# Up projection's seven-product tiles: products in more PSUM banks, closing sums last, two of the token sums split on GpSimd

## The chip, the cores and the metric

The kernel runs on one core of one Trainium2 chip. The metric is the device time of one execution in microseconds (us). Engines are named as the profile names them: PE is the TensorE matmul engine and PEld its weight load, DVE is VectorE, ACT is ScalarE, POOL is GpSimd, SP is SyncE, which issues the loads. Results of matmuls land in PSUM, which this kernel allots as eight banks of 128 partitions by 512 fp32.

## The reference

One layer of a hybrid network over 512 tokens of width 1024: a state-space mixer and a sparse attention mixer side by side, a feed-forward block with a causal convolution, and a gated embedding. What the change touches is the first half of the feed-forward block:

```
hid = rmsnorm(h, g_ffn) @ w_up          # 512x1024 @ 1024x5632
hid = causal_conv(hid, width 3) + conv_b
a, b = split(hid, 2)                     # 2816 columns each
h = h + (gelu(a) * b) @ w_down
```

All of it is fp32. The kernel splits every fp32 operand of a matmul into a high and a low part (high = the value rounded to the matmul's format, low = the rest) and sums three matmuls, high by high, high by low and low by high.

## The kernel before, in words

The stages before the feed-forward block (projections, state-space scan, attention, merge, output projection) end with the normed tokens `n2h`, `n2l` (high and low, 128 partitions by 8 row blocks by 512 tokens). The up projection then runs over 22 tiles `f` of 128 hidden columns; a tile makes the a-half and the b-half of its columns, each 128 by 512 tokens, in two PSUM banks called `ua` and `ub`.

**Plain tiles.** 17 of the 22 tiles load two raw weight blocks of 128 by 1024 (`wr`, three buffers), split each into `wh` and `wl` (two buffers each; the copy that makes the high part is always on ACT, the subtraction that makes the low part on DVE for the a-half and on POOL for the b-half), and run 8 times 3 matmuls of 512 columns into `ua`, then the same into `ub`.

**Seven-product tiles.** For `f` = 4, 6, 8, 10 and 12 (`SEVEN`) the function `up_seven` treats the tile as a 2 by 2 block product (a-half and b-half columns by the two halves of the 1024 rows, times the two token halves) and uses the Strassen-Winograd form: seven block products of 4 times 3 matmuls of 256 columns, in place of eight. Its inputs are sums of weight blocks, made for each tile in `weight_sums` (s1 to s4 in tiles `sf`, split into `sw`), and sums of token blocks, made once in `token_sums` during tile 1 (`nf`, split into `nt`). The products come in the order 1, 2, 6, 7, 5, 3, 4, each into half a bank (`H0` or `H1`, 256 columns). Products 1 and 7 share bank C, 6 is in bank D (both called `us`), products 2 and 3 share the a-bank `ua`, products 5 and 4 the b-bank `ub`. An ACT copy takes product 1 to `m1`; DVE sums make u2 = p6 + m1, u3 = p7 + u2, u4 = p5 + u2 (tiles `mu`), and four closing sums in place, p2 += m1, p5 += u3, p3 += u4, p4 += u3, leave the a-half in `ua` and the b-half in `ub`.

**After a tile** the function `convolved` reads both banks: ACT scales each into `cv`, DVE adds two shifted terms for each half (`scalar_tensor_tensor`, line 63), ACT applies gelu, POOL multiplies (later tiles in two pieces), ACT and DVE split the product into `ffp` (pairs of tiles 0 to 7) or `ffa` and `ffs` with more sums (from tile 8).

**PSUM.** The pool has four tags of two banks each: `acc`, `s`, `t` and `o`. A tag's two banks are taken in turn. `either()` gives `acc` and `o` in turn; every tile takes its `ua` bank from `either()` and its `ub` bank from `s`; a seven-product tile takes C and D from `t`.

**Order.** On PE the instructions run in the order of the program from tile 2 on (`manual_schedule`). On ACT, DVE, POOL and the load queue a planner orders them at build time: it simulates the engines, and takes among the ready instructions the one that stands earliest in the program. `issue_after(x)` puts the instructions traced within it behind `x` where both are on one engine. Once built, each engine runs its list strictly in that order and waits at the head for whatever is not there yet. A wait between engines on a PSUM tile covers the bank: the profile shows PE waiting for a sum in the other half of the bank that it is to write.

In the profile the splits show as line 75 (ACT copy) and line 54 (all `tensor_tensor`), matmuls as lines 82 to 84, the convolution's shifted terms as line 63, its scaled copy as line 1360 and gelu as line 1363.

Of the kernel before, what the change touches and what calls it, by code (L numbers as in the profile page):

```python
# [16 lines left out]
MUL, ADD, SUB = ALU.mult, ALU.add, ALU.subtract  # L17

P = 128
# [3 lines left out]
KD = D // P  # L23
# [21 lines left out]
def hybrid_kernel(ctx: ExitStack, tc: tile.TileContext, A, out):  # L45
    nc = tc.nc
    V, G, S, PE = nc.vector, nc.gpsimd, nc.scalar, nc.tensor
# [5 lines left out]
    def tt(o, a, b, op, e=V):  # L53
        e.tensor_tensor(o, a, b, op=op)  # L54
# [19 lines left out]
    def copy(o, a):  # L74
        S.activation(o, a, AF.Copy)  # L75

    def split(hi, lo, src, e=V):
        copy(hi, src)
        tt(lo, src, hi, SUB, e)

    def mm3(ps, lh, ll, rh, rl, start, stop):
        PE.matmul(ps, lh, rh, start=start, stop=False)  # L82
        PE.matmul(ps, lh, rl, start=False, stop=False)  # L83
        PE.matmul(ps, ll, rh, start=False, stop=stop)  # L84
# [15 lines left out]
    def bank(tag, name):  # L100
        return psp.tile([P, 512], F32, tag=tag, name=name, bufs=BANKS[tag])
# [71 lines left out]
    def last(engine):  # L173
        return next(i for i in reversed(nc.cur_bb.bb.instructions) if i.engine == engine)
# [3 lines left out]
    def either():  # L178
        turn[0] ^= 1
        return ("acc", "o")[turn[0]]  # L180

    def wraw(name, ld, row0, c0, kt, c, raw=None):

        if raw is None:
            raw = pw.tile([P, kt * c], F32, name="wr", tag="wr", bufs=3)
            raw = raw.rearrange("p (k c) -> p k c", k=kt)
        n = (row0 // (kt * P)) * (ld // c) + c0 // c
        nc.sync.dma_start(raw, dr(name, n * P * kt * c, [[kt * c, P], [c, kt], [1, c]]))
        return raw

    def wload(name, ld, row0, c0, kt, c, e=V, keep=None, raw=None):
        if raw is None:
            raw = wraw(name, ld, row0, c0, kt, c)
        if keep is None:
            hi = pw.tile([P, kt * c], F32R, name="wh", tag="wh").rearrange("p (k c) -> p k c", k=kt)
            lo = pw.tile([P, kt * c], F32R, name="wl", tag="wl").rearrange("p (k c) -> p k c", k=kt)
        else:
            hi, lo = keep
        split(hi, lo, raw, e)
        return hi, lo  # L200
# [506 lines left out]
    for lv in range(5):  # L707
        n = 1 << lv
        m = MID + n
        rotate([t[:, :, m:m + n] for t in tab], [t[:, :, MID:m] for t in tab], n, lv, [t[:, :, :n] for t in tabm], G)  # L710
    for t, c, sign in zip(tab, (COS, SIN), (1.0, -1.0)):
        S.activation(t[:, :, 0], c[:, 6], AF.Copy, scale=sign)
        x = t[:, :, HC - 1:HC]
# [308 lines left out]
    for hc in range(2):  # L1022
# [3 lines left out]
        for cc in range(2):  # L1026
            c = 2 * hc + cc
            ps = bank(either(), "glu")
# [169 lines left out]
    for d2 in range(4):  # L1198
        hi, lo = wload("w_br_nsa", D, 0, d2 * 256, 4, 256, V)
        for dd in range(2):  # L1200
            dt_ = 2 * d2 + dd
            ps = bank(either(), "br")
# [24 lines left out]
    for qp in range(2):  # L1227
        for hf, qt in ((0, 0), (0, 1), (1, 0), (1, 1)) if qp == 0 else ((0, 2), (1, 2), (0, 3), (1, 3)):
            cs = slice(hf * 512, hf * 512 + 512)
            qs_ = slice(qt * P, (qt + 1) * P)  # L1230
            ps = bank(either(), "wo")
# [109 lines left out]
    ups = {}  # L1341

    def up(f, t0, t1_):
        wab, pss = ups[f]
        for ab in range(2):
            hi, lo = wab[ab]
            for k in range(KD):
                mm3(pss[ab][:, t0:t1_], hi[:, k], lo[:, k], n2h[:, k, t0:t1_], n2l[:, k, t0:t1_],
                    k == 0, k == KD - 1)
# [16 lines left out]
    SEVEN = range(4, 13, 2)  # L1366
    K1, K2, H0, H1 = slice(0, 4), slice(4, 8), slice(0, HT), slice(HT, T)
    BT = {}

    def token_sums():  # L1370
        n = {}
        for ks, hs in ((K1, H0), (K2, H0), (K1, H1), (K2, H1)):
            t = Slot("nf", 2)
            tt(t.parts(4), n2h[:, ks, hs], n2l[:, ks, hs], ADD, G)
            n[ks.start, hs.start] = t
        n11, n21, n12, n22 = (t.parts(4) for t in n.values())
        tt(n11, n12, n11, SUB)
        tt(n12, n22, n12, SUB)
        tt(n22, n22, n11, SUB)
        tt(n21, n21, n22, SUB)  # L1380
        for m, x in ((6, n22), (7, n12), (5, n11), (4, n21)):
            w = 4 if m == 4 else 2
            BT[m] = [[Slot("nt", w // 2, F32R) for _ in range(4 // w)] for _ in range(2)]
            for i in range(4 // w):
                split(*(BT[m][y][i].parts(w) for y in range(2)), x[:, w * i:w * i + w])
        for t in n.values():
            t.done()

    def tokens(m, x, k):
        if m in BT:  # L1390
            w = 4 // len(BT[m][x])
            return BT[m][x][k // w].parts(w)[:, k % w]
        ks, hs = {1: (0, H0), 2: (4, H0), 3: (4, H1)}[m]
        return (n2h, n2l)[x][:, ks + k, hs]

    def weight_sums(f):
        raw = [wraw("w_up", 2 * DFF, 0, ab * DFF + f * P, KD, P) for ab in range(2)]
        a11, a12, a21, a22 = (r[:, ks] for r in raw for ks in (K1, K2))
        sf = [Slot("sf", 2) for _ in range(2)]
        (s1, s2), (s3, s4) = ([v.rearrange("p (k c) -> p k c", k=4) for v in (t.t[:, :512], t.t[:, 512:])] for t in sf)  # L1400
        tt(s1, a21, a22, ADD)
        tt(s2, s1, a11, SUB)
        tt(s3, a11, a21, SUB)
        tt(s4, a12, s2, SUB)
        wa = wload(None, 0, 0, 0, KD, P, V, raw=raw[0])
        wb = [pw.tile([P, 4, P], F32R, name=n, tag=n) for n in ("wh", "wl")]
        split(*wb, a22, G)
        hl = [[Slot("sw", 2, F32R) for _ in range(2)] for _ in range(2)]
        for i in range(2):
            split(hl[i][0].t, hl[i][1].t, sf[i].t, (V, G)[i])  # L1410
            sf[i].done()
        W = {1: [w[:, K1] for w in wa], 2: [w[:, K2] for w in wa], 4: wb}
        for m, (i, o) in {5: (0, 0), 6: (0, 4), 7: (1, 0), 3: (1, 4)}.items():
            W[m] = [t.parts(8)[:, o:o + 4] for t in hl[i]]
        return W, [t for x in hl for t in x]

    def up_seven(f):
        W, held = weight_sums(f)
        A, B = ups[f][1]
        C, D_ = (bank("t", "us") for _ in range(2))  # L1420
        ps = {1: C[:, H0], 2: A[:, H0], 6: D_[:, H0], 7: C[:, H1], 5: B[:, H1], 3: A[:, H1], 4: B[:, H0]}
        u = Slot("mu", 2)
        m1, u2, u3, u4 = (u.parts(4)[:, i] for i in range(4))

        def prod(m):
            for k in range(4):
                mm3(ps[m], W[m][0][:, k], W[m][1][:, k], tokens(m, 0, k), tokens(m, 1, k), k == 0, k == 3)

        prod(1)
        copy(m1, ps[1])  # L1430
        prod(2)
        tt(ps[2], ps[2], m1, ADD)
        prod(6)
        tt(u2, ps[6], m1, ADD)
        prod(7)
        tt(u3, ps[7], u2, ADD)
        prod(5)
        tt(u4, ps[5], u2, ADD)
        tt(ps[5], ps[5], u3, ADD)
        prod(3)  # L1440
        tt(ps[3], ps[3], u4, ADD)
        prod(4)
        tt(ps[4], ps[4], u3, ADD)
        for t in (*held, u):
            t.done()

    def up_tile(f):
        kept = []
        if f == 1:
            kept = [Slot(f"w1{n}", 2, F32R) for n in range(4)]  # L1450
        wab = []
        for ab in range(0 if f in SEVEN else 2):
            keep = [kept[2 * ab + x].parts(KD) for x in range(2)] if kept else None
            wab.append(wload("w_up", 2 * DFF, 0, ab * DFF + f * P, KD, P, (V, G)[ab], keep=keep))
        ups[f] = wab, [bank(either(), "ua"), bank("s", "ub")]
        if f == 0:
            up(0, 0, 256)
            return
        if f == 1:
            up(1, 0, 256)  # L1460
            up(0, 256, 512)
            convolved(0)
            up(1, 256, 512)
            for k_ in kept:
                k_.done()
            token_sums()
        elif f in SEVEN:
            up_seven(f)
            if f == SEVEN[-1]:
                for t in BT.values():  # L1470
                    for x in t:
                        for y in x:
                            y.done()
        else:
            up(f, 0, 512)
        convolved(f)
        if f >= NF - 2:
            free[2].append(cvs[f % 2])

    for f in range(2):  # L1480
        up_tile(f)
    with tc.manual_schedule(engines={mybir.EngineType.PE}):
        for f in range(2, NF):
            up_tile(f)
# [5 lines left out]
    b1, b2, u4, us_at = {}, {}, {}, {}  # L1490
    with tc.manual_schedule(engines={mybir.EngineType.PE}):
# [73 lines left out]
        for n, c in enumerate(range(NR, NP)):  # L1565
# [5 lines left out]
            x = [u[:, n % NSET] for u in (uh, ul)]  # L1571
# [296 lines left out]
```

## Time and profile before

| what | value |
|---|---|
| median of 3 runs | 807.33 us (806.28 to 808.7) |
| profiled execution, its own time | 806.57 us |
| its span, first to last instruction | 804.8 us |
| mean granted PE clock | 0.998 |
| PE busy | 787.4 us (98%), 4618 matmuls |
| DVE, ACT, POOL busy | 578.3, 416.2, 283.2 us |

Up projection in the span: tile 0 starts at 390.3 us, the first seven-product tile at 437.17 us, the last one ends at 541.85 us, the stage ends at about 640 us.

How to read it: all times inside the execution count from the first instruction of the span. In a timeline row the first number is the start, the second the length of the row, and a bracket at the end tells how long the engine sat idle before it and what it waited for. Rows of instructions that follow without a gap overlap a little, since they are pipelined. In a row of a view by stretches the pairs are busy time and, in brackets, the count of instructions of each engine.

### The profile page before, as it was taken

To read this page: it belongs to the slowest core of one execution; us is meant where nothing else is said; L and a number is where in the kernel's file an instruction comes from. 1 tells how busy PE (TensorE), PEld (TensorE's weight loads), DVE (VectorE), ACT (ScalarE), POOL (GpSimd) and SP (SyncE) were. 2 spreads that over 40 slices of the span, in tenths; PEclk is the share of its full clock that TensorE was granted. 3 is DMA by queue.
4 is the path that set the end of the run, shared out by engine and by line. 5 is a ranking of instruction groups with operands and counts; after the bars stand their busy time and mean duration, and the time that the engine had idled before them with its cause. 6 is when DMAs were issued, how large, how long until landed. Compare 5 with 4: busy or idle time off the path is not lost.

```text
span 804.8 us, 12548 instructions
## 1 busy us (share of the span) xinstructions
PE 787.4 (98%) x4618; PEld 671.5 (83%) x4618; DVE 578.3 (72%) x1156; ACT 416.2 (52%) x769; POOL 283.2 (35%) x302
## 2 busy tenths in 40 slices
PE   9999999999999999999999899899999999999996
PEld 8888888878888888878997788788888888888885
DVE  7988987976777730785599888885544757999753
ACT  6836554467767642443464554454443433484642
POOL 4576122137555433311354444553333200001222
PEclk9999999999999999999999999999999999999999
DMA  9973112243135123342032233234232352525111
GB/s 351 354 210 108 53 68 67 67 121 115 54 105 165 46 67 115 113 156 73 1 105 79 79 105 103 81 107 155 82 103 94 98 174 79 209 66 171 53 53 52
DMA packets 29854, 89.72 MB, mean 111 GB/s; under 512 B 3681, under 2 KB 6113, under 8 KB 29793
## 3 DMA queue, kind: packets, MB, share of 16 engines
q1 hardware_dynamic: 29216, 87.88, 33.0%
q10 hardware_dynamic: 576, 1.05, 0.3%
q8 instruction: 36, 0.59, 0.3%
q14 instruction: 26, 0.20, 0.1%
HBM read 79.48 MB, written 5.24 MB: 105 GB/s over the span
## 4 chain that ended last, share of the span: by engine, by line
PE 74%; DVE 14%; ACT 4%; issue 3%; POOL 2%; DMA 2%; POOLq 0%; ACTq 0%; DVEq 0%
PE pj L82 6%; PE pj L83 6%; PE pj L84 6%; PE p L83 3%; PE p L82 3%; PE p L84 3%; DVE wl L54 3%; PE ub L82 2%; PE sps L1068 2%; PE ub L83 2%; PE ub L84 2%; PE ua L83 2%; PE ua L82 2%; PE ua L84 2%; PE ptp L1088 2%
## 5 line engine op out<-in xcount | busy, mean ns | idle before, releaser
L54 POOL TENSOR_TENSOR wl<-wr,wh 128x1024 fp32r<-128x1024 f32 (+1 forms) x39 | 89.8, 2303 | 211.2 <-ACT wh L75 188.8
L75 ACT ACTIVATE wh<-wr 128x1024 fp32r<-128x1024 f32 x88 | 90.9, 1033 | 95.7 <-issue 28.6
L54 DVE TENSOR_TENSOR wl<-wr,wh 128x1024 fp32r<-128x1024 f32 x49 | 71.3, 1454 | 44.9 <-ACT wh L75 44.7
L82 PE MATMUL pj<-n1h,wh 128*128 128x512 f32 x224 | 91.0, 406 | 0.0
L83 PE MATMUL pj<-n1l,wh 128*128 128x512 f32 x224 | 87.7, 392 | 0.0
L84 PE MATMUL pj<-n1h,wl 128*128 128x512 f32 x224 | 87.5, 391 | 0.0
L63 DVE SCALAR_TENSOR_TENSOR cv<-ub,cols,cv 128x511 f32<-128x511 f32 (+1 forms) x44 | 32.9, 747 | 35.7 <-ACT cv L1360 35.0
L83 PE MATMUL ua<-n2l,wh 128*128 128x512 f32 (+1 forms) x156 | 57.0, 366 | 0.2 <-DVE n2l L63 0.2
L82 PE MATMUL ua<-n2h,wh 128*128 128x512 f32 (+1 forms) x156 | 57.1, 366 | 0.0
L84 PE MATMUL ua<-n2h,wl 128*128 128x512 f32 (+1 forms) x156 | 56.9, 365 | 0.0
L84 PE MATMUL ub<-n2h,wl 128*128 128x512 f32 (+1 forms) x136 | 51.3, 377 | 0.0
L83 PE MATMUL ub<-n2l,wh 128*128 128x512 f32 (+1 forms) x136 | 51.2, 377 | 0.0
L82 PE MATMUL ub<-n2h,wh 128*128 128x512 f32 (+1 forms) x136 | 51.2, 377 | 0.0
L84 PEld LDWEIGHTS pj<-n1h,wl 128*128 128x128 f32 x224 | 42.0, 188 | 8.9
L82 PEld LDWEIGHTS pj<-n1h,wh 128*128 128x128 f32 x224 | 42.1, 188 | 8.2 <-issue 0.4
L83 PEld LDWEIGHTS pj<-n1l,wh 128*128 128x128 f32 x224 | 42.2, 188 | 7.3 <-issue 0.2
L60 POOL TENSOR_SCALAR pr<-pr,su,gates 128x512 f32<-128x512 f32 (+2 forms) x64 | 39.1, 626 | 14.2 <-DVE su L1080 14.1
L75 ACT ACTIVATE ph<-ptp 128x128 fp32r<-128x128 f32 (+1 forms) x64 | 27.8, 435 | 25.9 <-PE ptp L1088 25.7
L54 DVE TENSOR_TENSOR pl<-ptp,ph 128x128 fp32r<-128x128 f32 (+1 forms) x64 | 31.0, 486 | 13.3 <-ACT ph L75 12.2
L54 POOL TENSOR_TENSOR cv<-cv 128x256 f32<-128x256 f32 (+1 forms) x22 | 26.6, 1209 | 31.0 <-DVE cv L63 26.7
L1079 ACT ACTIVATE pr<-pr,nb 128x512 f32<-128x512 f32 (+2 forms) x64 | 35.4, 557 | 0.7 <-DVE nb L1077 0.6
L1077 DVE CUSTOM_DVE_ANT_0 pr<-sps,maskb 128x512 f32<-128x512 f32 (+2 forms) x64 | 28.9, 488 | 8.4 <-PE ptp L1088 6.3
(529 smaller groups left out, 2276.1 us busy)
## 6 DMA issues: line engine op xcount, KB each, us to landing
wr<-in_w_up_dram SPq DMA_DIRECT2D x44, 512.0 KB, 3.5
wr<-in_w_in_dram SPq DMA_DIRECT2D x28, 512.0 KB, 3.7
b<-in_w_down_dram SPq DMA_DIRECT2D x14, 512.0 KB, 3.6
QQ<-QT SPq DMA_DIRECT2D x16, 256.0 KB, 4.6
wr<-in_w_out_dram SPq DMA_DIRECT2D x8, 512.0 KB, 3.4
wr<-in_w_down_dram SPq DMA_DIRECT2D x8, 512.0 KB, 4.2
wr<-in_w_ple_gate_dram SPq DMA_DIRECT2D x8, 512.0 KB, 3.5
xT<-in_x_t_dram SPq DMA_DIRECT2D x4, 512.0 KB, 9.8
```

What stands on the lines that cost most here:

```text
L54: e.tensor_tensor(o, a, b, op=op)
L60: e.tensor_scalar(o, a, s1, s2, op0=op0, op1=op1)
L63: e.scalar_tensor_tensor(o, a, s, b, op0=op0, op1=op1)
L75: S.activation(o, a, AF.Copy)
L82: PE.matmul(ps, lh, rh, start=start, stop=False)
L83: PE.matmul(ps, lh, rl, start=False, stop=False)
L84: PE.matmul(ps, ll, rh, start=False, stop=stop)
L1068: PE.matmul(o, self.QQ[:, x, qt * P:(qt + 1) * P], KK[:, :, self.g, :w] if both else KK[:, self.br, self.g, :w], start=x == 0, stop=x == 1)
L1077: V.tensor_tensor_reduce(out=pp, in0=ps, in1=maskb[:, T - w:], scale=-(HD ** -0.5), scalar=3e38, op0=ADD, op1=ALU.min, accum_out=nb)
L1079: S.activation(pp, pp, AF.Exp, bias=nb, scale=-1.0, accum_out=su)
L1088: PE.transpose(ps[:, (qt - kt) * P:(qt - kt + 1) * P], self.pr[qt][:, kt * P:(kt + 1) * P], ident)
```

## The change

Four edits.

1. `token_sums`: the low parts of the token sums for products 4 and 5 (three subtractions, two of 128 by 512 and one of 128 by 1024) move from DVE to POOL.
2. `weight_sums`: the load of `wa` (the split of the first raw block, which products 1 and 2 use) stands ahead of the four weight sums instead of behind them. For the first seven-product tile only, the ACT copies of the `sw` splits are put behind the ACT copy of `wa`.
3. `up_seven`: six banks in place of four. Product 7 goes to a bank of its own, E (from `either()`), product 3 to a bank of its own, X (from `s`), product 5 to the second half of C. `ua` holds product 2 alone and `ub` product 4 alone.
4. The closing sums: p2 + m1 stays in place in `ua`; p3 + u4 is read from X and written to the second half of `ua`; p5 + u3 is read from C and written to the second half of `ub`, after product 4 in the program; p4 + u3 stays in place and comes last.

```
-                split(*(BT[m][y][i].parts(w) for y in range(2)), x[:, w * i:w * i + w])
+                split(*(BT[m][y][i].parts(w) for y in range(2)), x[:, w * i:w * i + w], G if m in (4, 5) else V)
...
     def weight_sums(f):
         raw = [wraw("w_up", 2 * DFF, 0, ab * DFF + f * P, KD, P) for ab in range(2)]
         a11, a12, a21, a22 = (r[:, ks] for r in raw for ks in (K1, K2))
+        wa = wload(None, 0, 0, 0, KD, P, V, raw=raw[0])
+        wa_at = last(mybir.EngineType.Activation)
         sf = [Slot("sf", 2) for _ in range(2)]
...
         tt(s4, a12, s2, SUB)
-        wa = wload(None, 0, 0, 0, KD, P, V, raw=raw[0])
         wb = [pw.tile([P, 4, P], F32R, name=n, tag=n) for n in ("wh", "wl")]
         split(*wb, a22, G)
         hl = [[Slot("sw", 2, F32R) for _ in range(2)] for _ in range(2)]
         for i in range(2):
-            split(hl[i][0].t, hl[i][1].t, sf[i].t, (V, G)[i])
+            with tc.issue_after(wa_at) if f == SEVEN[0] else nullcontext():
+                split(hl[i][0].t, hl[i][1].t, sf[i].t, (V, G)[i])
...
     def up_seven(f):
         W, held = weight_sums(f)
-        A, B = ups[f][1]
+        X, E = bank("s", "us"), bank(either(), "us")
         C, D_ = (bank("t", "us") for _ in range(2))
-        ps = {1: C[:, H0], 2: A[:, H0], 6: D_[:, H0], 7: C[:, H1], 5: B[:, H1], 3: A[:, H1], 4: B[:, H0]}
+        A, B = ups[f][1] = [bank(either(), "ua"), bank("s", "ub")]
+        ps = {1: C[:, H0], 2: A[:, H0], 6: D_[:, H0], 7: E[:, H0], 5: C[:, H1], 3: X[:, H0], 4: B[:, H0]}
...
         prod(2)
-        tt(ps[2], ps[2], m1, ADD)
+        tt(A[:, H0], ps[2], m1, ADD)
...
         prod(5)
         tt(u4, ps[5], u2, ADD)
-        tt(ps[5], ps[5], u3, ADD)
         prod(3)
-        tt(ps[3], ps[3], u4, ADD)
+        tt(A[:, H1], ps[3], u4, ADD)
         prod(4)
-        tt(ps[4], ps[4], u3, ADD)
+        tt(B[:, H1], ps[5], u3, ADD)
+        tt(B[:, H0], ps[4], u3, ADD)
...
-        ups[f] = wab, [bank(either(), "ua"), bank("s", "ub")]
+        ups[f] = [wab, None if f in SEVEN else [bank(either(), "ua"), bank("s", "ub")]]
```

## The prediction, on record before the result

> **What bounds the kernel now.** I read the page first, then the stretches between the starts of the seven-product tiles, then what PE waits for in them, then the timelines around each wait. The page's first line and the stretches (span in us, then busy time and count of PE, PEld, DVE, ACT, POOL, then clock and DMA):
>
> ```profile
> PE 787.4 (98%) x4618; PEld 671.5 (83%) x4618; DVE 578.3 (72%) x1156; ACT 416.2 (52%) x769; POOL 283.2 (35%) x302
> ```
> ```profile
> 437.17:452.00 14.83, 10.87 (x85) 10.26 (x85) 11.32 (x14) 4.84 (x8) 6.66 (x4) 1.00 0.31 107
> 452.00:474.27 22.27, 21.38 (x135) 19.20 (x133) 19.22 (x25) 10.84 (x15) 10.21 (x5) 1.00 0.29 95
> 474.27:496.51 22.24, 21.34 (x134) 19.18 (x133) 19.09 (x24) 10.84 (x15) 10.20 (x5) 1.00 0.29 95
> 496.51:520.47 23.96, 21.61 (x135) 19.24 (x133) 21.23 (x32) 10.94 (x16) 11.45 (x7) 1.00 0.28 89
> 520.47:541.85 21.38, 21.24 (x135) 19.15 (x133) 17.97 (x29) 12.31 (x18) 11.83 (x7) 1.00 0.30 99
> 541.85:640.00 98.15, 98.15 (x435) 81.27 (x434) 52.98 (x82) 42.22 (x60) 34.61 (x27) 1.00 0.31 104
> ```
> ```profile
> PE ub L82 <- DVE ub L54: 4.9, 4, 1.9
> PE us L82 <- ACT mu L75: 1.7, 2, 1.3
> PE us L84 <- DVE wl L54: 1.5, 1, 1.5
> ```
>
> PE is the bound (98% busy, full clock), so a microsecond counts where PE stands still. The first stretch is tile 4 alone; the next four are each a plain tile and a seven-product tile of the same work, yet last 22.27, 22.24, 23.96 and 21.38 us. The last block is all that PE waits for in those stretches: 4.9 + 1.7 + 1.5 = 8.1 us, in seven waits. From 541.85 to 640 PE is busy without a gap, so time won before goes straight to the end.
>
> **The change part by part.** (1) *Products in their own banks.* The wait of product 4 in tile 6, and the DVE queue ahead of it:
>
> ```profile
> 472.73 0.38 PE L82 MATMUL ub<-nt,wh 128*128 128x256 f32 x1 [0.89 <-DVE ub L54]
> ```
> ```profile
> 468.47 2.27 DVE L54 TENSOR_TENSOR wl<-wr,wh 128x1024 fp32r<-128x1024 f32 x1
> ...
> 472.26 0.42 DVE L54 TENSOR_TENSOR ub<-ub,mu 128x256 f32<-128x256 f32 x1
> 474.16 1.29 DVE L54 TENSOR_TENSOR sf<-wr 128x512 f32<-128x512 f32 x2 [1.48 <-DMA wr<-in_w_up_dram]
> 475.37 0.43 DVE L54 TENSOR_TENSOR ua<-ua,mu 128x256 f32<-128x256 f32 x1
> ```
>
> Product 4 goes to the first half of the bank where DVE still sums product 5 in the second half, and that sum stands in DVE's queue behind a weight split of 2.27 us and the sums u2, u3 and u4. After the change the bank holds product 4 alone; nothing of DVE's is due in it before PE writes. The 4.9 us go. Product 7 likewise no longer waits for the ACT copy of product 1 (1.7 us), since it has bank E; product 5 now shares that bank and comes two products later:
>
> ```profile
> 488.17 0.28 PE L82 MATMUL us<-nt,sw 128*128 128x256 f32 x1
> 491.05 0.28 PE L82 MATMUL ub<-nt,sw 128*128 128x256 f32 x1
> ```
>
> Products 6 and 7 lie between these rows, so a product takes 2.88 / 2 = 1.44 us, and the copy has 1.44 us more before it is due. The first matmul after a wait takes 0.38 us against 0.28 here: 0.10 for each of seven restarts, 0.7 us. All waits together are worth 8.1 + 0.7 = 8.8 us. The count of DVE sums stays seven a tile; none is added.
>
> (2) *Tile 4.* One of the waits on DVE's sums (removed above), and these two, with what stood in the queues:
>
> ```profile
> 439.07 0.39 PE L84 MATMUL us<-n2h,wl 128*128 128x256 f32 x1 [1.48 <-DVE wl L54]
> 444.72 0.38 PE L82 MATMUL us<-nt,sw 128*128 128x256 f32 x1 [1.31 <-ACT mu L75]
> ```
> ```profile
> 433.78 1.06 ACT L75 ACTIVATE sw<-sf 128x1024 fp32r<-128x1024 f32 x1 [3.65 <-DVE sf L54]
> ...
> 436.00 1.05 ACT L75 ACTIVATE wh<-wr 128x1024 fp32r<-128x1024 f32 x1
> ...
> 442.58 0.63 ACT L1363 ACTIVATE cv<-cv 128x512 f32<-128x512 f32 x1 [3.98 <-DVE cv L63]
> ...
> 444.30 0.37 ACT L75 ACTIVATE mu<-us 128x256 f32<-128x256 f32 x1
> ```
> ```profile
> 437.08 1.94 DVE L54 TENSOR_TENSOR wl<-wr,wh 128x1024 fp32r<-128x1024 f32 x1 [0.29 <-ACT wh L75]
> ```
> ```profile
> 437.90 3.38 POOL L54 TENSOR_TENSOR sw<-sf,sw 128x1024 fp32r<-128x1024 f32 x1
> ```
> ```profile
> 431.58 0.39 PE L82 MATMUL ub<-n2h,wh 128*128 128x512 f32 x1
> ```
>
> The `wa` copy stood behind both `sw` copies on ACT, which had idled 3.65 us before them. Its buffer comes free when PE leaves the a-half of tile 3 at 431.58. Put first, the copy ends near 431.6 + 0.2 (for the last matmuls to end) + 1.05 = 432.9 and the low part by 432.9 + 1.94 = 434.8, before PE arrives at 437.17: the 1.48 us go. Behind it on ACT wait the two `sw` copies, and behind them POOL's split; the sums keep PE no earlier than product 6 at 437.17 + 2.88 = 440.05.
>
> What is late next is product 5, due at 437.17 + 4 x 1.44 = 442.93, while the ACT copy of product 1 ended at 444.30 + 0.37 = 444.67, behind a gelu that waited 3.98 us for DVE. If that stays, 1.74 us come back; if the queue is rearranged, nothing. POOL's split ends at 441.28, product 7 is due at 441.49: 0.2 us of room. I take 0.8 us of new waits in tile 4 (range 0 to 1.74).
>
> (3) *Starts of tiles 6, 8, 10, 12.* The same `wa` split in tile 8 has no room:
>
> ```profile
> 479.74 0.39 PE L82 MATMUL ub<-n2h,wh 128*128 128x512 f32 x1
> ...
> 485.44 0.39 PE L84 MATMUL us<-n2h,wl 128*128 128x256 f32 x1
> ```
> ```profile
> 481.66 1.05 ACT L75 ACTIVATE wh<-wr 128x1024 fp32r<-128x1024 f32 x1
> ```
> ```profile
> 480.82 1.22 DVE L54 TENSOR_TENSOR sw<-sf,sw 128x1024 fp32r<-128x1024 f32 x1
> ...
> 483.40 1.98 DVE L54 TENSOR_TENSOR wl<-wr,wh 128x1024 fp32r<-128x1024 f32 x1
> ```
>
> DVE ends the split at 483.40 + 1.98 = 485.38 and PE uses it at 485.44. With the wait of 0.89 us gone, PE comes about 1 us sooner. The buffer is free from 479.74, so the copy could start 1.9 us before 481.66, and the edit lets the planner take it before the `sw` work. If it does, nothing is lost; if not, about 1 us a tile is. I take 0.15 us for each of four starts, 0.6 (range 0 to 4).
>
> The `sw` low part has the cover: it ends at 482.04, product 6 needs it at 488.17.
>
> (4) *Token splits on POOL.* The rows for DVE's side and, nearest in shape, for POOL's:
>
> ```profile
> L54 DVE TENSOR_TENSOR nt<-nf,nt 128x512 fp32r<-128x512 f32 x6 | 4.3, 754 | 0.0
> L54 DVE TENSOR_TENSOR nt<-nf,nt 128x1024 fp32r<-128x1024 f32 x1 | 1.2, 1215 | 0.0
> ```
> ```profile
> L54 POOL TENSOR_TENSOR wl<-wr,wh 128x512 fp32r<-128x512 f32 x5 | 6.4, 1285 | 11.6 <-issue 5.2 <-PE ua L84 3.7 <-ACT wh L75 2.7
> L54 POOL TENSOR_TENSOR wl<-wr,wh 128x1024 fp32r<-128x1024 f32 x7 | 18.1, 2592 | 31.1 <-ACT wh L75 31.1
> ```
> ```profile
> 412.00:426.00 14.00, 14.00 (x85) 12.54 (x84) 13.96 (x18) 8.72 (x12) 2.41 (x2) 1.00 0.12 39
> ```
>
> DVE loses 2 x 0.754 + 1.215 = 2.72 us, POOL gains 2 x 1.285 + 2.592 = 5.16 us. From 412 to 426 DVE is busy 13.96 of 14.00 us and POOL 2.41, so it looks like relief. But these rows overlap:
>
> ```profile
> 453.49 2.78 DVE L54 TENSOR_TENSOR sf<-sf,wr 128x512 f32<-128x512 f32 x1
> ```
> ```profile
> 453.32 2.39 POOL L54 TENSOR_TENSOR wl<-wr,wh 128x1024 fp32r<-128x1024 f32 x1 [5.93 <-ACT wh L75]
> ```
>
> A DVE sum of 128 by 512 elements takes 2.78 us here; it ends 0.56 us after POOL's subtraction. DVE stood for about the length of it. If all of POOL's 5.16 us hold DVE, DVE is 5.16 - 2.72 = 2.44 us later; if none, 2.72 us earlier, of which PE, busy in full, gains nothing. DVE's split for tile 3 is just in time:
>
> ```profile
> 424.96 1.22 DVE L54 TENSOR_TENSOR wl<-wr,wh 128x1024 fp32r<-128x1024 f32 x1
> ```
> ```profile
> 426.14 0.39 PE L82 MATMUL ua<-n2h,wh 128*128 128x512 f32 x1
> ```
>
> It ends at 426.18; PE's first use of the low part, the third matmul, is at about 426.6. Of 2.44 us, 2.0 would reach PE. If half of POOL's 5.16 us hold DVE, 2.58, hold and relief cancel; that lies between the ends, and for the hold falling at the wrong moment I take 0.5 us (range 0 to 2.0).
>
> The Trainium skill, SBUF — State Buffer, section "Who interferes with whom", says that a DVE instruction with two SBUF inputs and a GpSimd instruction that reads SBUF lock each other out for a whole instruction. The pair of rows at 453 agrees. By that rule alone the sum below would carry 2.0 us for this edit in place of 0.5.
>
> (5) *Closing sums last.* They delay the convolution of the tile, not a matmul: the `ua` sum already ran at 475.37, and bank reuse comes a tile later. I take 0.
>
> **Sum.** -8.8 + 0.8 + 0.6 + 0.5 = -6.9 us. The profiled execution took 806.57 us (span 804.8 and 1.77 around it), which gives 799.7; the median of the runs shown lies 0.76 higher, so the forecast is 800.4 us.
>
> **The rivals.** *A, the side engines take over.* DVE is busy 19.22 of 22.27 us; ACT, DVE, POOL and the loads pass work around in a ring. If that ring keeps its pace, PE wins the waits inside tiles and loses 1 us at each of four starts (part 3), with 1.74 in tile 4: -8.8 + 4 + 1.74 + 0.5 = -2.6 us, 804.8. For it: the room of 0.06 us at 485.44, and the load that DVE waits for at 474.16. Against: the edit moves just this split forward, and the last stretch ran in 21.38 us with DVE at 17.97.
>
> *B, the token splits hold DVE for the lock.* Part 4 at its upper end and the rest as forecast: 800.4 + 1.5 = 801.9. By the rule of the Trainium skill named in part 4 (SBUF — State Buffer) the time would come out this way.
>
> *C, slower: the `s` banks.* A seven-product tile takes two `s` banks, so product 3's bank is the next plain tile's `ub`, and product 4's bank is the last plain tile's `ub`. In the rows above, the sum that empties the first would end at 475.80 and the next `ub` starts at 479.74: 3.9 us of room. If DVE's lag on the closing sums grows by more than 3.9 us, PE waits in every pair of tiles. With the forecast's gain of 6.9 spread over five tiles, it must cost 6.9 / 5 = 1.4 us a tile to be even, a lag of 5.3 us more; at 7 us more, each tile loses 3.1 us: -6.9 + 15.5 = +8.6, 816. Against: DVE idles 1.48 us at 474.16, so its lag should not build up.
>
> *D, the waits only move.* The planner may order DVE so that other operands are as late as those sums were: no change, 807.
>
> **How the numbers follow.** Forecast 0.60, A 0.14, B 0.10, C 0.08, D 0.08. The forecast's own range is 798 (all waits gone: 807.33 - 8.8 = 798.5, less the runs' spread) to 803. A reaches 805 and is taken in; C and most of D, under 0.2 together, are left out: 797.8 to 805.5. A run of this kernel tells about 0.3%, 2.4 us, from no change. Faster by more: forecast, B and most of A, 0.81. Within: D and the rest of A, 0.10. Slower: C and a little beside it, 0.09.
>
> **What would show it.** In the changed profile the three PE waits quoted second should be gone or below 2 us together, and the stretches of a plain and a seven-product tile should last 21.2 to 21.6 us each, tile 4 about 10.9. Rival A shows as PE waits on `wl` at the third matmul of tiles 6 to 12, B as waits on `wl` in tiles 2 and 3, C as a PE wait of `ub` or product 4 on a DVE sum or the convolution. The forecast is wrong if the seven-product stage is shorter by less than 3 us, or if PE gains there and loses it after 550 us.

## The result, and the profile after

The change made the kernel slower: 811.49 us median (809.75 to 813.43, 7 runs) against 806.93 us (7 runs) before, a ratio of 1.0052 with a 95% interval of 1.0036 to 1.0068. The forecast was 800.4 us and its range ended at 805.5. The profiled execution, which the views below show, took 812.18 us, 0.7 above the median.

The page of the changed kernel, its first engine line, and all that PE waits for from 400 to 560 us:

```profile
PE 789.2 (97%) x4618; PEld 673.5 (83%) x4618; DVE 580.4 (72%) x1153; ACT 416.8 (51%) x769; POOL 287.4 (35%) x305
```
```profile
PE us L84 <- DVE wl L54: 11.0, 4, 2.8
PE us L82 <- ACT mu L75: 0.6, 1, 0.6
PE ua L84 <- DVE wl L54: 0.4, 1, 0.4
```

The waits that the prediction wanted gone are gone: there is no row of product 4 waiting for a sum, and 0.6 us is left of the 1.7 us for the ACT copy. In their place stand four waits of 2.8 us at the third matmul of tiles 6, 8, 10 and 12, for the low part of the first weight split. The stretches that answer to those shown of before (tile 4 alone, then four pairs of a plain and a seven-product tile, then the rest of the stage; columns as there):

```profile
437.85:448.80 10.95, 10.32 (x85) 10.11 (x84) 9.52 (x12) 4.31 (x7) 7.28 (x4) 1.00 0.34 105
448.80:474.30 25.50, 22.69 (x134) 20.55 (x133) 19.70 (x25) 10.96 (x15) 9.53 (x5) 0.93 0.28 92
474.30:498.24 23.94, 21.23 (x134) 19.14 (x133) 19.42 (x22) 10.97 (x15) 10.03 (x5) 1.00 0.23 75
498.24:522.28 24.04, 21.28 (x135) 19.11 (x134) 19.61 (x30) 10.96 (x16) 10.79 (x7) 1.00 0.29 98
522.28:547.80 25.52, 22.76 (x135) 20.58 (x134) 22.25 (x33) 11.59 (x17) 10.78 (x7) 0.93 0.28 94
547.80:645.95 98.15, 98.15 (x435) 81.27 (x434) 53.77 (x83) 43.01 (x61) 34.66 (x27) 1.00 0.32 104
```

Tile 4 won 14.83 - 10.95 = 3.88 us. The four pairs lost 3.23, 1.70, 0.08 and 4.14 us, 9.15 in all. The stage starts 0.68 us later (437.85 against 437.17). Together +5.95 us, and the span grew by 810.5 - 804.8 = 5.7. The rest of the stage takes 98.15 us in both.

Two pairs, the first and the last, are 1.5 us longer than the two between, though the waits are alike; their granted clock is 0.93. The three microseconds after the wait of tile 6, and after that of tile 8:

```profile
463.00:466.00 3.00, 3.00 (x14) 3.00 (x15) 1.82 (x3) 0.63 (x1) 1.02 (x1) 0.50 0.54 178
...
489.00:492.00 3.00, 3.00 (x27) 3.00 (x26) 1.35 (x2) 1.08 (x2) 0.41 (x1) 1.00 0.58 180
```

After tile 6's wait PE ran at half clock and did 14 matmuls in the time of 27. The two pairs lose about 3 us by it together.

What made the first split late, in tile 8, from the timelines of PE, ACT, POOL and DVE of the changed kernel:

```profile
485.21 0.28 PE L82 MATMUL us<-n2h,wh 128*128 128x256 f32 x1
...
488.31 0.39 PE L84 MATMUL us<-n2h,wl 128*128 128x256 f32 x1 [2.71 <-DVE wl L54]
```
```profile
483.34 1.04 ACT L75 ACTIVATE wh<-wr 128x1024 fp32r<-128x1024 f32 x1
```
```profile
475.62 2.89 POOL L54 TENSOR_TENSOR wl<-wr,wh 128x1024 fp32r<-128x1024 f32 x1 [4.64 <-ACT wh L75]
482.20 2.40 POOL L54 TENSOR_TENSOR sw<-sf,sw 128x1024 fp32r<-128x1024 f32 x1 [3.68 <-ACT sw L75]
```
```profile
475.57 3.49 DVE L54 TENSOR_TENSOR sf<-wr 128x512 f32<-128x512 f32 x2 [1.90 <-DMA wr<-in_w_up_dram]
...
482.62 3.06 DVE L54 TENSOR_TENSOR sw<-sf,sw 128x1024 fp32r<-128x1024 f32 x1
485.60 1.52 DVE L63 SCALAR_TENSOR_TENSOR cv<-ub,cols,cv 128x511 f32<-128x511 f32 x2
487.04 1.22 DVE L54 TENSOR_TENSOR wl<-wr,wh 128x1024 fp32r<-128x1024 f32 x1
```

The high part is there at 484.38. DVE runs the low part only at 487.04, behind the low part of the weight sums and two terms of the convolution, as in the kernel before. The two `sf` sums (3.49 us against 1.29) start with POOL's split of the plain tile's b-half, and the `sw` split (3.06 against 1.22) starts after POOL's `sw` split. Each ends 0.5 to 1.1 us after POOL's.

The first of the two is no new loss. In the kernel before, the same split of POOL's (from 475.59) drew out the next sum instead, which takes 0.68 us at 479.32 in the changed kernel:

```profile
475.71 2.82 DVE L54 TENSOR_TENSOR sf<-sf,wr 128x512 f32<-128x512 f32 x1
...
485.31 1.52 DVE L63 SCALAR_TENSOR_TENSOR cv<-ua,cols,cv 128x511 f32<-128x511 f32 x2
487.24 0.69 DVE L54 TENSOR_TENSOR ffp<-cv,ffp 128x512 fp32r<-128x512 f32 x1 [0.41 <-ACT ffp L75]
```

The second is new. Before, DVE's `sw` split started 0.5 us ahead of POOL's (480.82 and 481.32) and was not drawn out; now POOL's starts first, 482.20 against 482.62. New is also the order of DVE's list behind the split:

```profile
488.17 0.74 DVE L63 SCALAR_TENSOR_TENSOR cv<-ua,cols,cv 128x511 f32<-128x511 f32 x1
490.11 0.69 DVE L54 TENSOR_TENSOR ffp<-cv,ffp 128x512 fp32r<-128x512 f32 x1 [1.19 <-ACT ffp L75]
490.72 0.74 DVE L63 SCALAR_TENSOR_TENSOR cv<-ua,cols,cv 128x510 f32<-128x510 f32 x1
```

The low part `ffp`, which waits for an ACT copy, now stands between the two convolution terms that the next gelu needs; before, both ran ahead of it. From the first sum to that gelu it takes 15.98 us (475.57 to 491.55), where it took 12.95 (474.16 to 487.11).

The ring that ties the tiles together shows in the chain of waits. The loads that start it, of the kernel before and after, one pair of tiles apart:

```profile
470.77 3.37 DMA wr<-in_w_up_dram
...
493.02 3.47 DMA wr<-in_w_up_dram
```
```profile
472.09 3.45 DMA wr<-in_w_up_dram
...
497.49 3.51 DMA wr<-in_w_up_dram
```

Before, one turn takes 22.25 us, the same as the pair of tiles on PE (22.27, 22.24). After, this one takes 25.40. Turns differ: counted from DVE's first sum, the three between tiles 6 and 12 take 24.74, 25.45 and 22.86 us, where they took 22.22, 22.36 and 22.61. A turn runs: the load of a seven-product tile's second raw block (its buffer is freed when DVE has split the a-half of the plain tile before), the weight sums, their splits, the convolution of the tile before, POOL's product, gelu, the next convolution, the next split of an a-half, the next load. In the kernel before, the chain of waits over this turn holds no work of PE's.

### The profile page after: what moved, and what is told of

It reads as the page before. It is cut to its first block, busy times and chain, and to the rows that moved or that the text cites. A ratio compares the mean times of both kernels' runs of the same rounds, so it can differ in the third digit from the quotient of the medians.

```text
span 810.5 us, 12553 instructions
## 1 busy us (share of the span) xinstructions
PE 789.2 (97%) x4618; PEld 673.5 (83%) x4618; DVE 580.4 (72%) x1153; ACT 416.8 (51%) x769; POOL 287.4 (35%) x305
## 4 chain that ended last, share of the span: by engine, by line
PE 73%; DVE 15%; DMA 4%; issue 3%; ACT 2%; POOL 1%; SPq 0%; POOLq 0%; ACTq 0%; DVEq 0%
PE pj L82 6%; PE pj L83 6%; PE pj L84 6%; PE p L84 3%; PE p L82 3%; PE p L83 3%; DVE cv L63 3%; PE ua L83 2%; DVE wl L54 2%; PE sps L1068 2%; PE ua L82 2%; PE ua L84 2%; PE ub L83 2%; PE ub L84 2%; PE ub L82 2%
## 5 line engine op out<-in xcount | busy, mean ns | idle before, releaser
L54 DVE TENSOR_TENSOR wl<-wr,wh 128x1024 fp32r<-128x1024 f32 x49 | 66.6, 1359 | 45.6 <-ACT wh L75 44.7
```

## The experiments

The planner makes new lists for every kernel, so that an edit of a line changes more than its own instructions; where that bears on a verdict, it is said.

**Which of the edits.** Three kernels undo part of the change, one does the other part alone.

```
e1: -  ..., x[:, w * i:w * i + w], G if m in (4, 5) else V)
    +  ..., x[:, w * i:w * i + w])
e2: -  wa = wload(...) ; wa_at = last(Activation)          # ahead of the sums
    -  with tc.issue_after(wa_at) if f == SEVEN[0] else nullcontext():
    +  wa = wload(...)                                      # behind the sums
e3: e1 and e2 together (banks and closing sums alone)
e4: the kernel before with edits 1 and 2 alone
```

> The changed kernel with the token splits back on VectorE (edit 1 undone). Theory (the ring of VectorE, ScalarE, GpSimd and loads sets the pace once PE no longer waits inside the seven-product tiles): the waits at the starts of tiles 6 to 12 stay near 2.8 us each, 809 to 812 us. Rival 1 (the token splits on GpSimd start a lag of VectorE that never heals): the tile-start waits go, 800 to 804 us.

> The changed kernel with the first weight split back behind the weight sums and without its order rule in tile 4 (edit 2 undone). Theory of the ring: the tile-start waits stay near 2.8 us, tile 4 may wait up to 1.5 us at its start again, 810 to 813 us. Rival 2 (moving the split put the planner's lists out of step): the waits at the starts go, 800 to 804 us.

> Edits 3 and 4 alone (banks and closing sums; token splits and first weight split as before). Theory of the ring: waits of 2.5 to 3 us at the starts of tiles 6 to 12, 809 to 813 us. Rivals 1 and 2: without their cause the banks keep their gain, 799 to 803 us.

> Edits 1 and 2 alone, products in four banks and closing sums as before. Theory of the ring: no new wait at tile starts, product 4 waits for VectorE about 1 us a tile as before, the start of tile 4 gains up to 1.5 us, 804 to 808 us. Rivals 1 or 2: the tile-start waits show here too, 810 us or more.

Measured, with the ratio to the kernel before: e1 811.42 us, 1.0054 [1.0039, 1.0069]; e2 811.69, 1.0061 [1.0046, 1.0076]; e3 810.98, 1.0056 [1.0039, 1.0072]; e4 806.83, 0.9998 [0.9988, 1.0008]. What PE waited for, in e3 and then in e4:

```profile
PE us L84 <- DVE wl L54: 9.6, 4, 2.8
```
```profile
PE ub L82 <- DVE ub L54: 4.0, 4, 1.9
PE us L82 <- ACT mu L75: 2.3, 2, 1.9
PE ua L84 <- DVE wl L54: 0.4, 1, 0.4
```

The loss is whole in the banks and the closing sums; the token splits and the moved weight split neither make it nor mend it. Rivals 1 and 2 of the expectations fall. The half clock is not needed for the loss either: in e2 the granted clock is 1.00 from 437 to 548 us, and PE waits 12.6 us in five waits on `wl`.

**Order, hold, or load.** Three kernels each touch one link of the ring in the changed kernel.

```
e5: -  with tc.issue_after(wa_at) if f == SEVEN[0] else nullcontext():
    +  with tc.issue_after(wa_at), tc.issue_after(wa_lo):   # wa_lo: wa's low part on DVE
e6: -  split(hl[i][0].t, hl[i][1].t, sf[i].t, (V, G)[i])
    +  split(hl[i][0].t, hl[i][1].t, sf[i].t, V)
f1: +  own = Slot("ws", 2) if len(free[2]) >= ROOM else None      # ROOM = 8
    -  raw = [wraw("w_up", ..., KD, P) for ab in range(2)]
    +  raw = [wraw("w_up", ..., KD, P, own.parts(KD) if own and ab else None) for ab in range(2)]
    ...
    +  if own: own.done()                                   # behind the split of a22
```

> The changed kernel, in which every seven-product tile (not only the first) has the ScalarE copies and the VectorE low part of the weight-sum splits behind those of the first weight split. Theory 1 (the lists' order makes the start late: VectorE runs the low part of the sums, held by GpSimd, and two convolution terms ahead of the split that PE waits for): the tile-start waits fall from 11 us to under 4 us in all, 800 to 805 us. Theory 2 (the ring of loads, VectorE, ScalarE and GpSimd is slower than PE whatever stands first): the wait moves to the sums' operands (products 6 and 7) or to the next tile, 808 us or more.

> The changed kernel with the second weight-sum split's low part on VectorE too, in place of GpSimd: 1.1 us more work for VectorE a tile, and no GpSimd instruction of 2.4 us beside the first one. If the hold of VectorE by that GpSimd split (3.06 us in place of 1.22) is what makes the tile starts late: the starts wait at least 1 us less each, 804 to 808 us. If the hold costs nothing on the path: VectorE's extra work shows, 812 us or more.

> The changed kernel with the second raw weight block of each seven-product tile loaded into a free buffer of its own, so that its load needs no longer wait until VectorE has split the a-half of the tile before. This takes the load out of the ring. If the ring with that load sets the pace: the weight sums run earlier, the tile-start waits fall below 4 us in all, 799 to 805 us. If only the order of the lists or the hold by GpSimd counts: 808 us or more.

e5: 810.06 us, 1.0044 [1.0028, 1.0060]. Putting the late split first made that wait shorter and gave as much back elsewhere:

```profile
PE us L84 <- DVE sw L54: 5.1, 4, 2.3
PE us L84 <- DVE wl L54: 3.6, 4, 1.2
PE us L82 <- ACT mu L75: 1.5, 3, 0.6
```

The sum is 10.2 us against 11.6 for the same kinds of rows in the changed kernel. Which of these two splits comes first is not the cause; whatever stands second is late (theory 2). The order of `ffp` and the convolution terms is the same in e5 as in the changed kernel, so e5 does not test it.

e6: 803.23 us, 0.9955 [0.9940, 0.9970], a little below the range expected. Five more splits of VectorE's made the kernel 1% faster than the changed one. DVE's `sw` splits in the changed kernel and in e6, and e6's wait:

```profile
L54 DVE TENSOR_TENSOR sw<-sf,sw 128x1024 fp32r<-128x1024 f32 x5 | 13.5, 2694 | 0.0
```
```profile
L54 DVE TENSOR_TENSOR sw<-sf,sw 128x1024 fp32r<-128x1024 f32 x10 | 12.8, 1324 | 0.0
```
```profile
PE us L84 <- DVE wl L54: 4.8, 4, 1.3
```

Ten splits on DVE take less time (12.8 us) than five did beside POOL's five (13.5). The tile-start waits fall from 2.8 to 1.3 us. POOL's work of 2.4 us a tile did not relieve DVE at all; in tiles 6 to 12 it held DVE's split for about 1.8 us (3.06 against 1.22). But two splits on DVE take 2.35 us in place of 3.06 for one, which is 0.7 us a tile and not the 8 us of this run. The planner's list differs too: the low part that PE wants runs one convolution term earlier, and both terms of the a-half stand ahead of `ffp` again (484.50, then 486.72). What hold and list are worth apart, e6 does not show.

f1: 800.52 us, 0.9927 [0.9910, 0.9943]. PE's waits of half a microsecond or more from 390 to 570 us are two, both in the plain tiles ahead of the first seven-product tile:

```profile
PE ua L84 <- DVE wl L54: 2.1, 1, 2.1
PE ua L84 <- DVE w L54: 1.4, 1, 1.4
```

With the load out of the ring the seven-product tiles run without a wait. The ring, with that load as a link, set the pace of the changed kernel.

**The one wait that was taken away.** f3 moves one line of the changed kernel back, so that product 4 waits for a sum in its bank again:

```
-        prod(4)
         tt(B[:, H1], ps[5], u3, ADD)
+        prod(4)
         tt(B[:, H0], ps[4], u3, ADD)
```

> The changed kernel with one line moved: the closing sum of product 5 stands before product 4 again, so that product 4 waits for it (same bank), while products 3, 5 and 7 keep their new banks. If the loss comes from taking away that one wait (PE then runs ahead of the ring and GpSimd's splits fall on VectorE's sums): the wait of product 4 is back, the tile-start waits shrink below 5 us in all, 805 to 809 us. If it comes from the banks or from sums that now read one bank and write another: the tile-start waits stay and product 4's wait comes on top, 812 us or more.

807.23 us, 0.9995 [0.9986, 1.0005]: the whole loss is gone with one line. Its waits, and DVE's instructions in tile 8:

```profile
PE ub L82 <- DVE ub L54: 5.8, 4, 2.6
PE us L82 <- ACT mu L75: 0.5, 1, 0.5
PE ua L84 <- DVE wl L54: 0.4, 1, 0.4
```
```profile
474.27 1.30 DVE L54 TENSOR_TENSOR sf<-wr 128x512 f32<-128x512 f32 x2 [1.53 <-DMA wr<-in_w_up_dram]
...
480.88 1.22 DVE L54 TENSOR_TENSOR sw<-sf,sw 128x1024 fp32r<-128x1024 f32 x1
```

Product 4's wait is back and no tile waits at its start. The banks and sums from one bank to another cost nothing by themselves. In tile 8 DVE's rows are those of the kernel before again: the `sw` split is short, POOL's other split draws out one sum (2.77 us at 475.81), and both convolution terms run ahead of `ffp` (485.37, then 487.29). In tile 6 POOL's `sw` split starts 0.19 us before DVE's, which is still held (3.30 us from 457.31), with both terms ahead of `ffp`; from first sum to first sum that turn takes 23.36 us, the next one 22.32. So an estimate from these two turns is that the hold of the `sw` split costs about 1 us a turn, and that the larger part of the 2.5 to 3.1 us of the changed kernel's two long turns goes to the list around it. No run changes that list alone, and whether the moment at which PE ends the tile or the order of the lists keeps POOL's split off DVE's is not told apart.

**Both together.** The buffer is left to tiles 6 to 12 (f5), given to the kernel before (f2 as in f1, f6 as in f5), and joined with e6's edit (f7).

```
f5, f6: own = Slot("ws", 2) if f > SEVEN[0] and len(free[2]) >= ROOM else None
f7:     f5 and   split(hl[i][0].t, hl[i][1].t, sf[i].t, V)
```

> The kernel before with the same free buffer for the second raw block. If the ring sets the pace there too: the waits for VectorE's sums shorten, 800 to 805 us. If PE's own waits on the banks set it: 805 to 808 us.

> The kernel before with the free buffer in tiles 6 to 12 only. Theory: with the ring loosened, PE's own waits for the banks (4.9 us for product 4) are what is left; they stay in part, 802 to 806 us, so that banks and buffer are each worth little alone and 7 us or more together. If the ring alone was the bound: as fast as the changed kernel with the same buffer.

> The changed kernel with the free buffer for the second raw block in tiles 6 to 12 only, not in tile 4, whose early sums delayed the splits of tiles 1 and 3 by 3.5 us. Theory of the ring: no waits at the starts of tiles 6 to 12, none inside them, and the 3.5 us gone too, 796 to 799 us. If the early sums of tile 4 were needed to get ahead of PE: waits at tile starts come back, 801 us or more.

> The changed kernel with the free buffer in tiles 6 to 12 and, besides, the second weight-sum split's low part on VectorE in place of GpSimd. If the hold of VectorE by that split matters only because it lies in the ring: with the ring loosened it wins nothing more, 798 to 801 us. If the hold costs by itself: about 3 us or more less than with the buffer alone, under 797 us.

The kernel before with the buffer is slower than without: f2 811.65 us, 1.0064 [1.0049, 1.0079], and f6 809.93 us, 1.0034 [1.0022, 1.0045]. Neither expectation held. f6's largest group of PE's waits, and DVE's list ahead of the sum that product 4 waits for in tile 4:

```profile
PE ub L82 <- DVE ub L54: 8.2, 4, 4.1
```
```profile
447.82 0.41 DVE L54 TENSOR_TENSOR mu<-us,mu 128x256 f32<-128x256 f32 x1
448.15 0.67 DVE L54 TENSOR_TENSOR sf<-sf,wr 128x512 f32<-128x512 f32 x1
448.75 0.68 DVE L54 TENSOR_TENSOR sf<-wr,ws 128x512 f32<-128x512 f32 x1
...
451.23 1.21 DVE L54 TENSOR_TENSOR sw<-sf,sw 128x1024 fp32r<-128x1024 f32 x1
452.36 0.42 DVE L54 TENSOR_TENSOR ub<-ub,mu 128x256 f32<-128x256 f32 x1
```

With the early loads the planner puts weight sums of the next seven-product tile and their split between u2 and the closing sum, and product 4 waits 8.2 us in all where it was 4.9. In f2, where tile 4 has the buffer too, the same kind of sums stand ahead of tile 3's split, and PE waits 5.7 us for it. So the buffer alone does not help while product 4 waits for that list; the banks alone do not help while the load is in the ring.

The changed kernel with the buffer gains: f5 799.59 us, 0.9903 [0.9882, 0.9923], between its two expected ranges, and f7 798.17 us, 0.9887 [0.9870, 0.9903], within the range expected if the hold matters only in the ring. In f5 no seven-product tile waits at its start; a wait of 2.0 us for POOL's split in tile 5 is new. f7's pairs of tiles:

```profile
460.71:481.69 20.98, 20.98 (x133) 19.09 (x132) 17.93 (x26) 11.45 (x16) 7.51 (x4) 1.00 0.33 107
481.69:502.68 20.99, 20.99 (x134) 19.09 (x133) 18.23 (x26) 11.01 (x16) 8.06 (x5) 1.00 0.25 82
502.68:523.65 20.97, 20.97 (x133) 19.08 (x132) 18.16 (x28) 10.83 (x16) 7.26 (x6) 1.00 0.26 84
523.65:544.63 20.98, 20.98 (x133) 19.09 (x132) 14.79 (x27) 10.70 (x18) 7.95 (x7) 1.00 0.44 142
```

PE is busy for the whole of every pair. With the ring loosened, taking POOL's split away brought 1.4 us, and the two intervals overlap, so that it may be nothing; inside the ring the same edit brought 8 us (811.49 to 803.23). The profiles of f5 and f7 differ by the wait in tile 5, 2.0 us and 0.7, and by a granted clock of 0.50 behind it in f5, from 457 to 460 us. f7 beats the kernel before by 1.1%, f5 by 1.0%.

## Why the prediction was wrong, step by step

**Part 1, the waits inside the tiles:** right as far as it went. The waits went from 8.1 us to 0.6. The error was to count them as a gain of 8.8 us. The turn of the ring before is 22.25 us without any work of PE's, and PE's own work in a pair is 21.38: the 0.89 us that PE waited for product 4 are the time by which the ring is longer, so they could move but not go unless the ring became shorter. In f3 this one wait, with the lists that come with it, makes the difference between 811.49 and 807.23 us.

**Part 2, tile 4:** right. Tile 4 took 10.95 us where about 10.9 was named, and the wait that came instead (0.6 us on the ACT copy, product 5) is the one that was priced at 0.8.

**Part 3, the starts of tiles 6 to 12:** this is the step that failed. It took 0.6 us, at most 4. It cost 11.0 us of waits and about 3 us of half clock after two of them. The prediction saw the 0.06 us of room and named the very split. Its upper price, about 1 us a tile, is the time by which PE would come earlier, and so it has the ring keep its 22.25 us. The ring did not keep it: in two turns it took 24.74 and 25.45. In tile 8 POOL's split drew out DVE's `sw` split by 1.8 us, and `ffp` stood between two convolution terms that the ring needs. Which share each has is an estimate (f3), not shown by a run of its own. The prediction also hoped that the moved edit would let the planner put the split first. The planner did not do so in tiles 6 to 12, and e5, which forces it, shows that it would not have helped.

**Part 4, the token splits:** right. The wait in tile 3 was 0.4 us against 0.5 taken, and e1 shows no difference within its interval.

**Part 5, the closing sums last:** priced at nothing, as delaying no matmul. That price was wrong: putting the sum of product 5 before product 4 again is all that f3 does, and the loss is gone.

**The rivals.** A, with 0.14, came nearest in kind: the side engines took over, by waits on `wl` at the third matmul as it said. But it has the ring keep its pace and the kernel gain, so its 804.8 us lack the two terms above, the slower ring and the half clock. Its sentence of evidence against, that the last stretch ran in 21.38 us, was misread: in that pair the weight sums of tile 12 began before the pair did, at 519.13, and the last of them started at 521.61, before POOL's split at 521.79, so none was held. It was the exception, not the rule. B did not show: 0.4 us of wait in tile 3, none in tile 2, and no gain in e1. D, the waits only move, had the move right, but the waits grew, from 8.1 to 12.0 us. C did not show: no wait of `ub` or of product 4 on a sum or the convolution. By the test named at the end (the seven-product stage shorter by less than 3 us) the forecast is wrong: the stage is 5.3 us longer (104.68 us before, 109.95 after).

The number forecast, 800.4, is what the change gives once the ring has slack: 800.52 in f1, 799.59 in f5.

The hold itself was in the prediction, from one pair of rows and the Trainium skill (SBUF — State Buffer, section "Who interferes with whom"), but weighed only for the token splits. The rule that two such instructions shut each other out agrees with e6's rows, 1.32 us in the mean for a split without POOL's beside it against 2.69 with it.

## What to carry to other kernels

A wait of the bound engine may be the time by which a loop of other engines is longer than the bound engine's own work. Before pricing its removal as a gain, follow the chain of waits once around. Where no piece of that loop is work of the bound engine, the loop is a second bound (here 22.25 us from load to load against 21.38 us of PE's work), and the gain comes only with a cut in the loop, here a buffer that takes a load out of it. That two engines keep the same pace does not tell which of them sets it; what the loop holds does. Where a planner makes new lists for each kernel, compare them too. Look also at which instructions of DVE and POOL will run side by side after the shift, not only before it.

## What the runs showed of the hardware that was not expected

PE's clock fell to half for some microseconds after waits that were not long: after 2.81 us in tile 6 of the changed kernel, but not after 2.71 us in tile 8; after 1.77 us in f3 (granted clock 0.50 from 451.5 to 454), but not after the wait of 1.92 us that ended at 518.94 in the kernel before (1.00 from 519 to 522). f3's rows:

```profile
449.45 0.38 PE L82 MATMUL ub<-nt,wh 128*128 128x256 f32 x1 [1.77 <-DVE ub L54]
```
```profile
451.50:454.00 2.50, 2.50 (x7) 1.92 (x7) 2.50 (x6) 2.29 (x3) 1.50 (x1) 0.50 0.00 0
```

The length of the wait alone does not decide it; what does was not tried. The Trainium skill, TensorE: Matmul & The Clock Gate, section "Part 1: The HAM clock gate (the "warmup" mystery)", gives half rate after at least one idle window of about 3.4 us that runs freely. The half rate agrees. The length does not: here waits from 1.77 us on were enough at times.

And GpSimd's subtraction on data in SBUF relieved VectorE of nothing: five of them cost VectorE as much as doing the work itself (13.5 us for five splits with POOL's five beside them, 12.8 us for all ten).
